# Moving the mixing of a channel group from the values' tile into the first tile of the next head pair's period

## The chip, the cores and the metric

One core of a Trainium2 chip runs the kernel. The metric is device time in microseconds. TensorE (PE) multiplies matrices, VectorE (DVE) and ScalarE (ACT) do elementwise work, GpSimd (POOL) a little of it, SyncE (SP) issues all the DMAs of this kernel.

## What is computed

One layer of a hybrid decoder works on 1024 prompt positions and 8 x 4 sample positions, 1056 token columns in all (T). One input projection gives the rows of two branches: 16 heads of attention and 8 channel groups of a gated position mixing. The output projection follows, then the residual and a norm. Cut to what matters here:

```python
z = rms_norm(x, norm_g) @ w_in
q, k, v, ga, u, vc, gb = split(z)
vc = layer_norm(gelu(vc), ln_g, ln_b);  u = gelu(u)
o_attn = dilated_attention(rope(q), rope(k), v)
# mixing of group g: positions s of a chunk of 128 to positions t, lower triangle only
mixed = einsum('gts,bcsgk->bctgk', w_s * tril, vc_chunks) + b_s
y = x + concat([o_attn * silu(ga), u * mixed * silu(gb)]) @ w_out
```

The sample positions open a chunk of their own, so they are mixed with the first 4 x 4 corner of `w_s`.

## The kernel before

**Tiles of the projections.** `w_in` is cut into 56 tiles of 128 output columns and `w_out` into 16. A tile is computed in three chunks of 352 token columns (`proj_chunk`, L190). Operands are split into a high and a low f16 half, and a chunk is 16 x 3 = 48 matmuls of 128x128 by 352 into one of three PSUM banks called `proj`. The weights of the next tile are split in four parts by ACT and DVE (`w_split`, L145 and L146: `wh`, `wl`) from `wraw`, which SP loads in two halves (L127). One tile of PE's work takes some 21 us.

**Side work.** Every 6 matmuls `proj_chunk` calls `fill` (24 calls a tile). It runs what is due in `timeline`, a list of (position, function), where the position counts tiles from the period's start. This side work is the prompt's attention (scores L634 and L635, mask and maximum L643, transposes of the probabilities by DMA L671, products L682 and L689, `onat` L694, transpose of the result L700), the sample's attention on the cached keys and values (`kvr` loaded at L735, split into `kvh` and `kvl` on ACT L743, DVE L746 or POOL L745, scores L774, `stsb` L763 and L782, mask L797), and the mixing. A scheduler of the framework then places instructions by priority and by which buffers are free, so that what is emitted later can stand earlier; the order on each engine is fixed when the program is built. The rotation (`rope`) is emitted at a higher priority.

**Periods.** `period(p)` handles head pair p-1 (g = p-1) beside the tiles that pair p and group g need. Its tiles are G (the gate `ga` of the pair), U (`u` of the group, into the tile `gb`), B (silu of `gb`, multiplied into the same tile `gb`), V (the values of pair p), and then X and Y, the two rotated halves of the queries and keys, by `run_ab`. Period 1 has U, B, V, X, Y; periods 2 to 5 have G, U, B, V, X, Y; period 6 has G, U, V, X, Y; period 7 has G, B, V, X, Y; period 8 has G, U, B, U, B. After Y, `rope` (L484) multiplies each chunk with cosines and sines (L490 to L497, reading two `proj` banks), splits it (`qkhl`, L153 and L154), and stores it (L498, L506, L507); L512 and L516 copy the sample's columns; `stack_load` (L518) reads queries and keys back (`qst`, `khd`, `klo`).

**The mixing.** For group g, `mix_load` issues 11 DMAs: eight of the normalised rows (`vr`, L886, two buffers of four DMAs each), `vrs` (L895), the triangle's weights `wr` (L896) and the bias `bb` (L897). `mix_prep` masks and splits the weights (`wm`). `mix(g, 0)` and `mix(g, 1)` each take a `proj` bank, do 12 matmuls (L913 to L915), add the bias (L927) and multiply by `gb` (L928) on DVE, split the result into `chl` (ACT L153, DVE L154) and store it to `act_d` (L935). `mix(g, 2)` does the same for the 32 sample columns (3 matmuls, L920 to L922). It needs the tile `gb` whole, so it comes after B of its group and before U of the next one writes that tile.

**Where the mixing stands before the change.** In periods 1 to 5 `period` calls `mix_load(g)` at once and puts the four steps at the start, 0.12, 0.45 and 0.79 of the values' tile. Period 6 has none. Period 7 does so for group 5, the period before's. Period 8 mixes group 6 in its last but one and last tiles, and group 7 is mixed after the periods.

Of the kernel before, what the change touches and what calls it, by code (L numbers as in the profile page):

```python
# [23 lines left out]
NP = H // 2  # L24
# [30 lines left out]
def hybrid_step_kernel(  # L55
# [50 lines left out]
    def bank(p, tag):  # L106
        return p.tile([128, 512], F32, tag=tag, name=tag)
# [220 lines left out]
    for qd in range(4):  # L328
        p = bank(ps_p, "proj") if qd < 3 else bank(ps_o, "o")
# [10 lines left out]
    for i in range(NQ + 1):  # L340
        if i + 3 <= NQ:
            x_load(i + 3)
        t0, n = TILES[i]
# [539 lines left out]
    def vr_load(g, half):  # L883
        vr = ap_.tile([128, 4, 2, 128], F16, tag="vr", name="vr", bufs=2)
        for i in range(4):
            SP.dma_start(out=vr[:, i], in_=vr_d[half * 4 + i, :, :, g * 128:(g + 1) * 128])  # L886
        return vr

    def mix_load(g):
        vr = [vr_load(g, 0), vr_load(g, 1)]  # L890
        vrs = ap_.tile([NS, 2, 128], F16, tag="vrs", name="vrs", bufs=1)
        wr = ap_.tile([128, 160], F32, tag="wr", name="wr", bufs=1)
        bb = ap_.tile([128, 160], F32, tag="bb", name="bb", bufs=1)
        gs = slice(g * 128, (g + 1) * 128)
        SP.dma_start(out=vrs, in_=vr_d[NQ, 0:NS, :, gs])  # L895
        SP.dma_start(out=wr, in_=wst[g])  # L896
        SP.dma_start(out=bb, in_=bst[g].partition_broadcast(128))  # L897
        mixs[g] = (vr, vrs, wr, bb)

    def mix_prep(g):  # L900
        vr, vrs, wr, bb = mixs[g]
        wm = ap_.tile([128, 2, 160], F16, tag="wm", name="wm", bufs=1)
        DVE.tensor_tensor(out=wr, in0=wr, in1=trl, op=ALU.mult)
        hilo(wr, wm[:, 0], wm[:, 1], SWS)
        mixs[g] = (vr, vrs, wm, bb)
# [31 lines left out]
    def mix_steps(g, direct=False):  # L937
        return [
            (0.1, lambda: mix_prep(g)),
            (0.7, lambda: mix(g, 0, direct)),  # L940
            (0.7, lambda: mix(g, 1, direct)),
            (0.1, lambda: mix(g, 2, direct)),
        ]
# [24 lines left out]
    def period(p):  # L968
        g = p - 1
        pr, ahl = prompt_steps(g)  # L970
        tiles = []
        if g > 0:
            tiles.append((MG[g], ga_evac))
        if p < NP - 1:
            tiles.append((MU[g], u_evac))
        if p < NP - 2:
            tiles.append((MGB[g], gb_evac))
        if p == NP - 1:
            tiles.append((MGB[g - 1], gb_evac))
        if p == NP:  # L980
            tiles += [(MU[g - 1], u_evac), (MGB[g - 1], gb_evac), (MU[g], u_evac), (MGB[g], gb_evac)]
        n = len(tiles)
        if p < NP:
            tiles.append((MV[p], v_evac(p)))
            n = len(tiles) + 2
        end = n - 0.85 if p < NP else n - 0.5
        ev = at(pr, 0.65, end)
        s0 = 0.4 if g == 0 else 0.0
        ev += [(s0 + t * (n - s0), f) for t, f in sample_steps(g, ahl)]
        mg = None  # L990
        if p < NP - 2:
            mg = g
        elif p > NP - 2:
            mg = g - 1
        if mg is not None:
            mix_load(mg)
            if p < NP:
                ready = len(tiles) - 1
                pos = (ready - 0.02, ready + 0.12, ready + 0.45, ready + 0.79)
            else:  # L1000
                pos = (2.95, 3.06, 3.4, 3.72)
            ev += [(t, f) for t, (_, f) in zip(pos, mix_steps(mg))]
        if p < NP:
            ev += at(v_trs(p), end + 0.25, end + 0.5)
        ev.sort(key=lambda e: e[0])
        timeline.extend(ev)
        now[0] = 0.0
        for i, (m, evac) in enumerate(tiles):
            w_load(m + 2)
            last = p == NP and i == n - 1  # L1010
            if last:
                mix_load(g)
            sp = [(i + 0.15 + 0.2 * q, lambda q=q: w_split(m + 1, q)) for q in range(4)]
            if p == NP or i < len(tiles) - 1:
                timeline.extend(sp)
            else:
                timeline.extend([(i + 0.15 + 0.2 * q, lambda q=q: w_split(MA[p], q)) for q in range(4)])
            timeline.sort(key=lambda e: e[0])
            for ci, (c0, w) in enumerate(CHUNKS):
                evac(proj_chunk(m, c0, w), c0, w)  # L1020
                if last:
                    if ci == 2:
                        while timeline:
                            timeline.pop(0)[1]()
                    act_load(slice(0, 7), c0, w)
                    act_load(slice(8, 15), c0, w)
        if p < NP:
            w_load(MB[p] + 1)
            for q in range(4):
                w_split(MB[p], q)  # L1030
            run_ab(p, None)
        assert not timeline
        now[0] = None
        if p == NP:
            for c0, w in CHUNKS:
                act_load(slice(7, 8), c0, w)

    for p in range(1, NP + 1):
        period(p)
# [294 lines left out]
```

## Time and profile before

| | |
|---|---|
| median of three runs | 1815.75 us (1815.25 to 1816.78) |
| the profiled execution | 1814.15 us |
| its span | 1812.2 us |
| its mean granted TensorE clock | 0.997 |
| busy in it: PE, DVE, ACT, POOL | 1778.8, 1069.9, 719.1, 118.1 us |

The span reaches from the first instruction of the profiled execution to the last; its time has some 2 us around that. Matmuls are pipelined: a row's duration is longer than the distance to the next one, so PE's pace is read from the starts. A row of a timeline has the start, the duration, the engine, the line of the kernel, the operation, its output and inputs, and in brackets how long the engine had been idle and what released it. Waits are listed as engine and instruction, then what ended the wait: total us, times, longest.

The periods begin, by the trace, at about 292 (period 1), 446, 600, 754, 907, 1060 (period 6), 1190 (period 7) and 1325 us (period 8); the first of the tiles' matmuls run some microseconds ahead of that, beside the rotation's end.

### The profile page before, as it was taken

How to read it: one execution, taken by the hardware profiler on the slowest of the kernel's cores; microseconds unless marked ns; L12 is line 12 of the kernel's file. 1: busy time of each engine (PE TensorE's matmuls, PEld its weight loads, DVE VectorE, ACT ScalarE, POOL GpSimd, SP SyncE). 2: the span in 40 equal slices, each digit the busy share in tenths (PEclk: the TensorE clock that was granted, in tenths of full speed). 3: DMA queues.
4: the chain of work that ended last, by engine and by line, in shares of the span. 5: the costliest groups of instructions: out<-in, count | busy, mean ns of one | idle time of the engine just before them, and what ended most of it. 6: DMA issues, size and time to landing. Idle time of an engine off the chain costs nothing. (4 is left out here: it accounts for less than half of the span.)

```text
span 1812.2 us, 37265 instructions
## 1 busy us (share of the span) xinstructions
PE 1778.8 (98%) x15040; PEld 1223.4 (68%) x15040; DVE 1069.9 (59%) x2383; ACT 719.1 (40%) x1605; POOL 118.1 (7%) x139
## 2 busy tenths in 40 slices
PE   8999999999999999999999999999999999999997
PEld 7866666666666666666666666666666666666677
DVE  7733595775766576477557657657657533434343
ACT  7522322642543444254344345445345311312133
POOL 0000020110010010001001000001001000000001
PEclk9999999999999999999999999999999999999999
DMA  7443337786667658567767866767765992333314
GB/s 269 104 102 70 78 116 213 160 183 179 160 141 171 166 123 197 157 158 149 174 157 143 176 182 150 177 189 160 185 177 124 241 340 79 71 79 80 81 42 192
DMA packets 340415, 276.13 MB, mean 152 GB/s; under 512 B 255890, under 2 KB 291730, under 8 KB 338130
## 3 DMA queue, kind: packets, MB, share of 16 engines
q1 hardware_dynamic: 340242, 273.76, 59.7%
q8 instruction: 117, 1.92, 0.4%
q14 instruction: 56, 0.45, 0.1%
HBM read 179.85 MB, written 38.26 MB: 120 GB/s over the span
## 5 line engine op out<-in xcount | busy, mean ns | idle before, releaser
L196 PE MATMUL proj<-xh,wh 128*128 128x352 f16 (+3 forms) x3712 | 1106.5, 302 | 4.2 <-ACT wh L145 1.2
L196 PE MATMUL proj<-xl,wh 128*128 128x352 f16 (+3 forms) x3712 | 1106.1, 302 | 1.4 <-DVE xl L154 1.4
L196 PE MATMUL proj<-xh,wl 128*128 128x352 f16 (+3 forms) x3712 | 1105.9, 302 | 0.3 <-DVE wl L146 0.3
L196 PEld LDWEIGHTS <-wh 128*128 128x128 f16 x7424 | 696.4, 98 | 324.1 <-issue 4.4
L196 PEld LDWEIGHTS <-wl 128*128 128x128 f16 x3712 | 362.3, 98 | 172.2 <-issue 1.7
L146 DVE SCALAR_TENSOR_TENSOR wl<-wraw,wh 128x512 f16<-128x512 f32 x288 | 191.7, 693 | 136.0 <-ACT wh L145 135.9
L145 ACT ACTIVATE wh<-wraw 128x512 f16<-128x512 f32 x288 | 167.3, 620 | 184.3 <-PE proj L196 178.8
L746 DVE SCALAR_TENSOR_TENSOR kvl<-kvr,kvh 128x896 f16<-128x896 f32 x128 | 142.2, 1111 | 69.7 <-ACT kvh L743 53.5
L655 ACT ACTIVATE sp<-sp,mn 128x256 f32<-128x256 f32 (+7 forms) x128 | 99.0, 774 | 169.7 <-DVE mn L643 169.7
L154 DVE SCALAR_TENSOR_TENSOR pn<-sp,pn 128x512 f16<-128x512 f32 (+2 forms) x192 | 111.9, 593 | 66.4 <-ACT pn L153 65.4
L745 POOL TENSOR_SCALAR kvh<-kvr 128x896 f16<-128x896 f32 x64 | 63.5, 993 | 781.0 <-DVE r L662 338.7
L153 ACT ACTIVATE pn<-sp 128x512 f16<-128x512 f32 (+2 forms) x192 | 96.7, 518 | 42.3 <-DMA pt<-pn 36.2
L743 ACT ACTIVATE kvh<-kvr 128x896 f16<-128x896 f32 x64 | 60.4, 944 | 85.2 <-issue 37.2
L643 DVE CUSTOM_DVE_ANT_0 sp<-s,mp 128x512 f32<-128x512 f32 (+3 forms) x128 | 74.7, 584 | 24.0 <-PE s L635 24.0
L154 DVE SCALAR_TENSOR_TENSOR yhl<-proj,yhl 128x352 f16<-128x352 f32 (+1 forms) x42 | 21.4, 510 | 84.0 <-ACT yhl L153 84.0
L153 ACT ACTIVATE yhl<-proj 128x352 f16<-128x352 f32 (+1 forms) x42 | 18.7, 446 | 125.6 <-PE proj L196 96.5
L682 PE MATMUL o<-vst,pt 128*128 128x128 f16 x576 | 66.1, 220 | 1.4 <-DVE onat L694 1.3
L634 PE MATMUL s<-khd,qst 128*128 128x512 f16 (+2 forms) x192 | 62.6, 326 | 3.0 <-DVE mn L643 2.9
L689 PE MATMUL o<-vst,pt 128*128 128x64 f16 x576 | 62.7, 193 | 0.0
L635 PE MATMUL s<-klo,qst 128*128 128x512 f16 (+2 forms) x192 | 60.2, 326 | 0.6 <-DMA klo<-k_d 0.6
L693 ACT ACTIVATE ot<-o,r 128x64 f32<-128x64 f32 x128 | 38.7, 302 | 42.4 <-PE o L689 42.3
L682 PEld LDWEIGHTS <-pt 128*128 128x128 f16 x576 | 52.5, 99 | 4.0
(191 smaller groups left out, 1505.2 us busy)
## 6 DMA issues: line engine op xcount, KB each, us to landing
wraw<-in_w_in SPq DMA_DIRECT2D x110, 512.0 KB, 4.8
kvr<-in_kc SPq DMA_DIRECT2D x64, 448.0 KB, 3.8
kvr<-in_vc SPq DMA_DIRECT2D x64, 448.0 KB, 3.8
wraw<-in_w_out SPq DMA_DIRECT2D x32, 512.0 KB, 4.9
yn<-in_x SPq DMA_DIRECT2D x8, 1024.0 KB, 12.9
out_y_p<-yn SPq DMA_DIRECT2D x16, 512.0 KB, 3.5
xn<-in_x SPq DMA_DIRECT2D x7, 1024.0 KB, 6.2
out_v_o<-tb SPq DMA_DIRECT2D x24, 176.0 KB, 3.7
```

The costliest lines, as they stand in the source:

```text
L145: ACT.activation(out=hi[:, sl, :], in_=r[:, rs, :], func=AF.Copy, scale=WS)
L146: DVE.scalar_tensor_tensor(out=lo[:, sl, :], in0=r[:, rs, :], scalar=WS, in1=hi[:, sl, :], op0=ALU.mult, op1=ALU.subtract)
L153: ACT.activation(out=hi, in_=src, func=AF.Copy, scale=scale)
L154: DVE.scalar_tensor_tensor(out=lo, in0=src, scalar=scale, in1=hi, op0=ALU.mult, op1=ALU.subtract)
L196: PE.matmul(out=ps[:, 0:n], lhsT=a[:, k, :], rhs=b[:, k, c0:c0 + n], start=(i == 0), stop=(i == 3 * KT - 1))
L634: PE.matmul(out=ps[:, 0:n], lhsT=qst[h][:, tq], rhs=khd[h][:, j0:j0 + n], start=True, stop=False)
L643: DVE.tensor_tensor_reduce(sp[:, j0:j0 + n], ps[:, 0:n], mp[:, S - nk + j0:S - nk + j0 + n], 1.0 / (QS * KS), prev, ALU.add, ALU.min, mn,)
L655: ACT.activation(out=sp[:, 0:nk], in_=sp[:, 0:nk], func=AF.Exp, scale=-1.0, bias=prev, accum_out=den)
L682: PE.matmul(out=o[:, 0:128].rearrange("p (l c) -> p l c", l=2), lhsT=pt[:, j], rhs=vst[:, :, kb, h * HD:(h + 1) * HD], start=(kb == 0), st ...
L689: PE.matmul(out=o[:, 0:64], lhsT=pt[:, w + j], rhs=vst[:, 0, kb, h * HD:(h + 1) * HD], start=False, stop=(kb == nb - 1))
L745: POOL.tensor_scalar(hi, r, VS, 1.0, ALU.mult, ALU.mult)
L746: DVE.scalar_tensor_tensor(out=lo, in0=r, scalar=KS if j < DB else VS, in1=hi, op0=ALU.mult, op1=ALU.subtract)
```

## The change

```diff
-        mg = None
-        if p < NP - 2:
-            mg = g
-        elif p > NP - 2:
-            mg = g - 1
-        if mg is not None:
-            mix_load(mg)
-            if p < NP:
-                ready = len(tiles) - 1
-                pos = (ready - 0.02, ready + 0.12, ready + 0.45, ready + 0.79)
-            else:
-                pos = (2.95, 3.06, 3.4, 3.72)
-            ev += [(t, f) for t, (_, f) in zip(pos, mix_steps(mg))]
+        if 1 <= g <= NP - 3 or p == NP:
+            m0 = g - 1 if g <= NP - 3 else NP - 3
+            ev += [(t, f) for t, (_, f) in zip((0.02, 0.07, 0.4, 0.73), mix_steps(m0))]
+        if g <= NP - 4 or p == NP - 1:
+            ev.append((n - 2.3, lambda: mix_load(g if g <= NP - 4 else NP - 3)))
+        if p == NP:
+            ev.append((1.2, lambda: mix_load(NP - 2)))
+            ev += [(t, f) for t, (_, f) in zip((2.95, 3.06, 3.4, 3.72), mix_steps(NP - 2))]
```

Groups 0 to 4 are now mixed in the G tile of periods 2 to 6, and group 5 in that of period 8, each with its steps at 0.02, 0.07, 0.4 and 0.73 of the tile. Their loads are called 0.7 into the values' tile of the period before (n counts the tiles with X and Y). In period 8 the loads of group 6 are called at 1.2 and its mixing stays. Nothing else is edited; lines behind 987 stand 5 lower. What is computed is the same.

The order of the built program shows what the scheduler made of it. The first place is DVE in the values' tile of period 1, behind the split of a weight part (`wl`, L146). Before, with the first part of the mixing of group 0 (L927, L928 and `chl`) among scores, probabilities (`pn`) and weights:

```order
L927 SCALAR_TENSOR_TENSOR proj<-proj,bb 128x512
L782 TENSOR_TENSOR stsb<-v,sa 128x4x7x8
L928 TENSOR_TENSOR proj<-proj,gb 128x512
L662 RECIPROCAL r<-den 128x1
L154 SCALAR_TENSOR_TENSOR pn<-sp,pn 128x512
L154 SCALAR_TENSOR_TENSOR pn<-sp,pn 128x128
L154 SCALAR_TENSOR_TENSOR chl<-proj,chl 128x512
L146 SCALAR_TENSOR_TENSOR wl<-wraw,wh 128x512
```

And now:

```order
L782 TENSOR_TENSOR stsb<-v,sa 128x4x7x8
L146 SCALAR_TENSOR_TENSOR wl<-wraw,wh 128x512
L662 RECIPROCAL r<-den 128x1
L146 SCALAR_TENSOR_TENSOR wl<-wraw,wh 128x512
L154 SCALAR_TENSOR_TENSOR pn<-sp,pn 128x512
L154 SCALAR_TENSOR_TENSOR pn<-sp,pn 128x128
L746 SCALAR_TENSOR_TENSOR kvl<-kvr,kvh 128x896
```

Three operations of the mixing are gone from there, and the same work as before follows in nearly the same order, up to L797.

The second place is DVE at the end of the rotation's third chunk, at the start of period 2 (the same at the other five boundaries). Before, the rotation's L497 was followed by a weight part, the split `qkhl`, and the copies L512 and L516:

```order
L495 TENSOR_TENSOR ta<-proj,cos_t 128x352
L496 TENSOR_TENSOR tb<-proj,sin_t 128x352
L146 SCALAR_TENSOR_TENSOR wl<-wraw,wh 128x512
L497 TENSOR_TENSOR o_5583<-ta,tb 128x352
L146 SCALAR_TENSOR_TENSOR wl<-wraw,wh 128x512
L154 SCALAR_TENSOR_TENSOR qkhl<-o_5583,qkhl 128x704
L512 COPY qbd<-qkhl 32x16x4
L516 COPY knw<-qkhl 32x64
```

And now:

```order
L495 TENSOR_TENSOR ta<-proj,cos_t 128x352
L496 TENSOR_TENSOR tb<-proj,sin_t 128x352
L146 SCALAR_TENSOR_TENSOR wl<-wraw,wh 128x512
L497 TENSOR_TENSOR o_5531<-ta,tb 128x352
L927 SCALAR_TENSOR_TENSOR proj<-proj,bb 128x512
L146 SCALAR_TENSOR_TENSOR wl<-wraw,wh 128x512
L154 SCALAR_TENSOR_TENSOR qkhl<-o_5531,qkhl 128x704
L928 TENSOR_TENSOR proj<-proj,gb 128x512
L512 COPY qbd<-qkhl 32x16x4
L516 COPY knw<-qkhl 32x64
```

The mixing's first two operations stand on both sides of `qkhl`; its `chl` follows the eight copies, ahead of L218, the first chunk of G. On PE the 12 matmuls of part 0 now follow 18 matmuls of that tile, those of part 1 come 42 matmuls of the tile later, and those of part 2 another 48 later. By the program's semaphores the first matmul of part 0 waits for L495 of the rotation's third chunk, part 1 for `chl` of part 0, and part 2 for L218 of the tile's second chunk.

The third place is SP behind the loads of `stack_load` at the same boundary. Before:

```order
L524 DMA klo_2716<-k_d_62 64x1024
L127 DMA wraw<-in_w_in 128x1024
L671 DMA_TRANSPOSE pt<-pn 128x2x128
L735 DMA kvr<-in_kc 128x896
L671 DMA_TRANSPOSE pt<-pn 128x2x128
L735 DMA kvr<-in_kc 128x896
```

And now:

```order
L524 DMA klo_2716<-k_d_62 64x1024
L935 DMA act_d<-chl 256x1x512
L127 DMA wraw<-in_w_in 128x1024
L886 DMA vr<-vr_d 128x2x128
L671 DMA_TRANSPOSE pt<-pn 128x2x128
L886 DMA vr<-vr_d 128x2x128 x2
L935 DMA act_d<-chl 256x1x512
L886 DMA vr<-vr_d 128x2x128 x4
L735 DMA kvr<-in_kc 128x896
L935 DMA act_d<-chl 256x1x32
L671 DMA_TRANSPOSE pt<-pn 128x2x128
L895 DMA vrs<-vr_d 32x2x128
```

The loads that the code calls in the values' tile stand here, as soon as the buffers of the group before come free; the first of the eight stands ahead of L498 of the rotation's third chunk. At the start of period 1, where the buffers are free, the eight `vr` loads and their three companions stood ahead of `wraw` and of all `kvr`; now one `wraw` and two `kvr` stand ahead of them, and the others lie among further `wraw` and `kvr`.

## The prediction

> **What bounds the kernel now.** The profiled execution took 1814.15 us, its span is 1812.2; the median of the three runs is 1815.75, 1.60 above the profiled one. The sum below is made against 1814.15, and the forecast is that sum plus 1.60. On this kernel a difference of 0.2% (3.6 us) is about what a measurement can tell from none.
>
> I read the page first. It names the engine.
>
> ```profile
> span 1812.2 us, 37265 instructions
> ...
> PE 1778.8 (98%) x15040; PEld 1223.4 (68%) x15040; DVE 1069.9 (59%) x2383; ACT 719.1 (40%) x1605; POOL 118.1 (7%) x139
> ```
>
> PE works 98% of the span. The change removes no matmul, so all that it can win is PE's idle time (and time at a lower clock), and all that it can lose is new idle time. So the second view is the list of PE's waits; its columns are total, times, longest.
>
> ```profile
> PE t L700 <- DVE mn L797: 3.8, 2, 3.5
> PE s L634 <- DVE mn L643: 2.9, 5, 0.9
> ...
> PE t L700 <- DVE onat L694: 2.1, 3, 1.0
> ...
> PE o L682 <- DVE onat L694: 1.3, 3, 0.8
> PE v L774 <- DVE stsb L763: 1.2, 1, 1.2
> ```
>
> The third view cuts the span by period (1, 3 and 7; columns: stretch and length, then PE, PEld, DVE, ACT, POOL busy, granted clock, DMA share, GB/s).
>
> ```profile
> 292.00:446.30 154.30, 147.47 (x1277) 99.71 (x1276) 99.99 (x235) 67.12 (x148) 12.40 (x13) 0.99 0.74 180
> ...
> 600.30:753.60 153.30, 152.96 (x1330) 103.88 (x1329) 97.88 (x232) 65.45 (x146) 11.18 (x13) 1.00 0.65 160
> ```
> ```profile
> 1190.50:1324.60 134.10, 131.91 (x1186) 89.99 (x1185) 91.01 (x222) 61.66 (x137) 10.64 (x13) 1.00 0.71 175
> ```
>
> Period 3 leaves PE idle for 0.3 us in 153. What can be won lies in period 1 and period 7.
>
> **Removed: the mixing in the values' tile.** In period 1 the worst stall stands in that tile: PE reaches L700 at 364.4 and gets on at 367.9, when DVE has read the bank in L797. DVE works without a pause until then, and the mixing is in its queue (start, duration, what):
>
> ```profile
> 359.91 0.69 DVE L927 SCALAR_TENSOR_TENSOR proj<-proj,bb 128x512 f32<-128x512 f32 x1
> ...
> 360.92 0.69 DVE L928 TENSOR_TENSOR proj<-proj,gb 128x512 f32<-128x512 f32 x1
> ...
> 362.38 0.69 DVE L154 SCALAR_TENSOR_TENSOR chl<-proj,chl 128x512 f16<-128x512 f32 x1
> ...
> 367.22 0.64 DVE L797 CUSTOM_DVE_ANT_0 ss<-t,msk,mn 64x416 f32<-64x416 f32 x1
> ```
>
> Each of the three holds DVE some 0.63 us (start to start), 1.9 together, and the order shows none of them ahead of L797 any more. L797 then ends 1.9 sooner. PE comes sooner too, because its 12 mixing matmuls ahead of the wait are gone:
>
> ```profile
> 354.60 0.22 PE L913 MATMUL proj<-wm,vr 128*128 128x128 f16 x1
> ...
> 355.27 0.17 PE L774 MATMUL v<-qbd,kvh 128*128 128x16 f16 x1
> ...
> 592.91 0.31 PE L196 MATMUL proj<-xh,wh 128*128 128x352 f16 x1
> ...
> 595.60 0.31 PE L196 MATMUL proj<-xh,wh 128*128 128x352 f16 x1
> ```
>
> The 12 take 0.67 us. They are done elsewhere at the same price, so they change the stall and not the sum of the work. The stall becomes 3.5 - 1.9 + 0.7 = 2.3: a gain of 1.2. Bounds: nothing, if another operand holds L797; 3.5, if the queues behind it thin out as well, since the loads of vr and the stores of chl leave this tile too.
>
> The clock follows the stall:
>
> ```profile
> 364.40:367.90 3.50, 0.01 (x1) 0.00 (x0) 3.35 (x11) 2.24 (x5) 0.17 (x1) 1.00 0.66 160
> 367.90:369.10 1.20, 1.17 (x15) 0.92 (x16) 1.20 (x3) 1.20 (x4) 0.00 (x0) 1.00 0.92 191
> 369.10:372.50 3.40, 3.40 (x22) 2.40 (x20) 2.41 (x7) 1.38 (x4) 0.00 (x0) 0.50 1.56 308
> ```
> ```profile
> 321.00:324.00 3.00, 1.83 (x25) 1.22 (x23) 1.37 (x9) 1.89 (x8) 0.00 (x0) 1.00 0.44 138
> 324.00:328.00 4.00, 4.00 (x43) 2.79 (x42) 3.78 (x9) 4.00 (x10) 0.00 (x0) 1.00 0.28 50
> ```
>
> For 3.4 us the clock is 0.50, which loses 1.7 us. The drop comes 1.2 us after the gap has ended, so the stretch of the same length ahead of it (365.7 to 369.1) was idle for only 2.2 us. A gap of 1.2 (at 321.5) brought no drop. A gap of 2.3 lies between the two, so the gain is between 0 and 1.7, and I take the middle, 0.85. The Trainium skill ("TensorE: Matmul & The Clock Gate", section "What's actually happening") says that the rate halves after at least one idle window of about 3.4 us, in windows that run free of the program; by that a gap of 2.3 brings no drop, the gain is 1.7 and the sum 0.85 better. The trace agrees with the length of the slow stretch (3.4 us) but shows the drop after a window that was idle for two thirds of it, so the rule is not my value, but a rival.
>
> Two smaller waits behind the stall hang on the same backlog, as do those of L682 in the list (1.3 in all, the longest in period 5) and two in period 7, where group 5 was mixed:
>
> ```profile
> PE s L634 <- DVE mn L643: 0.6, 2, 0.4
> ```
> ```profile
> PE o L682 <- DVE onat L694: 0.8, 1, 0.8
> ```
> ```profile
> PE s L634 <- DVE mn L643: 0.9, 1, 0.9
> PE t L700 <- DVE onat L694: 0.6, 1, 0.6
> ```
>
> The first fence is 355 to 380 us, the second 907 to 1061, the third 1240 to 1324.6. I take two thirds of each, since what comes next on DVE is close behind: 0.4, 0.9 and 1.0. Bounds: nothing, and all of it (0.6, 1.3, 1.5).
>
> **Moved: the loads of group 0.** In the order, period 1 now issues weights and two key tiles ahead of them. Before, these waited 7.0 us on SP:
>
> ```profile
> 296.54 5.18 SPq L886 DMA_DIRECT2D vr<-vr_d  x8
> 301.77 0.62 SPq L895 DMA_DIRECT2D vrs<-vr_d  x1
> ...
> 303.06 0.43 SPq L897 DMA_DIRECT2D bb<-in_bst  x1
> 303.54 1.72 SPq L127 DMA_DIRECT2D wraw<-in_w_in  x1
> ```
>
> That helps a wait of 0.8 us for L643 at 318.5, whose DVE queue stands behind a late key tile:
>
> ```profile
> 316.99 0.95 ACT L743 ACTIVATE kvh<-kvr 128x896 f16<-128x896 f32 x1 [3.23 <-DMA kvr<-in_kc]
> ```
> ```profile
> 317.97 1.09 DVE L746 SCALAR_TENSOR_TENSOR kvl<-kvr,kvh 128x896 f16<-128x896 f32 x1 [2.65 <-ACT kvh L743]
> 318.98 0.28 DVE L643 CUSTOM_DVE_ANT_0 sp<-s,mp 128x128 f32<-128x128 f32 x1
> ```
>
> But the first key tile's split (0.95 on ACT, then 1.09 on DVE) now stands ahead of a quarter of the next weights (L145, L146) in both queues, so that a late key tile holds up weights.
>
> ```profile
> kvr<-in_kc SPq DMA_DIRECT2D x64, 448.0 KB, 3.8
> ```
>
> Issued near 298, it lands near 302 (3.8 us in the page's list of DMAs); its split costs PE between nothing and its own 2.0. I take the gain of 0.8 less 0.4, so 0.4 (bounds 2.0, with L774's wait of 1.2 gone too, and -1.2).
>
> **Added: mixing in the first tile of the next period, at six places** (starts of periods 2 to 6 and 8). Its first matmul now follows 18 matmuls of that tile, so at 595.60 in period 3 (0.149 us each from 592.91). The bank that it is given is the one that the rotation's third chunk reads in L495:
>
> ```profile
> 593.11 0.53 DVE L491 TENSOR_TENSOR tb<-proj,sin_t 128x352 f32<-128x352 f32 x1 [4.15 <-PE proj L196]
> ...
> 595.27 0.52 DVE L495 TENSOR_TENSOR ta<-proj,cos_t 128x352 f32<-128x352 f32 x1
> ...
> 598.16 0.89 DVE L154 SCALAR_TENSOR_TENSOR qkhl<-o,qkhl 128x704 f16<-128x704 f32 x1 [0.30 <-ACT qkhl L153]
> ...
> 600.77 0.52 DVE L218 SCALAR_TENSOR_TENSOR sg<-ta,proj 128x352 f32<-128x352 f32 x1 [0.21 <-ACT ta L217]
> ```
>
> L495 ends at 595.79: PE waits 0.19, and some 0.05 to be told (L797 ended at 367.86, PE went on at 367.9): 0.24. Queued behind it on PE are all the matmuls of the tile, so this is on the path: 6 x 0.24 = 1.4 (bounds 0 and 0.5 each, 3.0). DVE's own part of the mixing is hidden: L927 and the others fill pauses, and push qkhl to 598.6 at most. The second part waits until chl of the first has been split, which I reckon for 602.2 (598.6 + 0.9 for qkhl, 1.5 for the copies between it and L218, 0.6 for L928, 0.6 for chl), against PE's arrival at 595.60 + 0.24 + 0.67 + 42 x 0.149 = 602.8: 0.6 to spare. The third has about the same. If that cover is gone, each microsecond past it is paid six times.
>
> On SP, 11 loads and 3 stores move to the tile in which the rotated keys are stored and read back:
>
> ```profile
> L886 SPq DMA_DIRECT2D vr<-vr_d x64: 524/602/1985, 296.5 to 1416.4; - x64
> ```
>
> At 0.6 us each, the stores counted like the loads, that is 8.4 us of SP's time per boundary. By the order one load stands ahead of the stores of queries and keys; it waits for the first part's matmuls (596.5), and those stores have nothing to store before qkhl is split. Seven loads and two stores stand ahead of the first cached key tile, some 5.4 us. The stores of chl are read in the last projections only. PE has spare time there: its first use of the stored keys is pushed by the mixing itself (0.9 at each part). I cost this at nothing, bounds 0 and 1 us a boundary (6).
>
> **The sum:** gains 1.2 + 0.85 + 0.4 + 0.9 + 1.0 + 0.4 = 4.75; cost 1.4. Net -3.35: profiled 1810.8, median 1812.4.
>
> **Rivals.** (a) *The stall moves and little is won.* DVE's work in that tile is the same but for 1.9 us, and L797 waits for the scores as well; then the 3.5 and the clock's drop stay (2.05 of the gain), and the net is -1.3: 1814.4. For it: DVE is busy for 3.35 of the 3.5 us. Against it: the order puts nothing else ahead of L797. (b) *Slower: the chain of the mixing misses the bank at the boundaries.* Place: the second and third part in the first tile of six periods. L927 waits for PE, stands ahead of qkhl on DVE, and ACT must split too; from 0.6 us beyond my reckoning on, PE stands. At 0.7 us on either part, 6 x 1.4 = 8.4, net +5.05: 1820.8. For it: the margins are only reckoned, and SP's and ACT's queues are new there. Against it: DVE is idle for 4.15 us ahead of L491, so it has no backlog there. (c) *The whole stall goes* with the lighter queues: 2.3 more of stall and 0.85 of clock, net -6.5: 1809.2. (d) *No drop at a gap of 2.3*: the clock slows only after a gap longer than 2.3 us, which the rows (a drop at 3.5, none at 1.2) allow; 0.85 better, 1811.6. That is the Trainium skill's rule above. (e) *The change doesn't do what it says:* the loads are put into the values' tile in the code, but the order has them in the next period's first tile. Had they stood where the code says, SP would have 11 x 0.6 = 6.6 us less there; since that is costed at nothing, the time is that of the forecast, and its chance is within it.
>
> **How the numbers follow.** Forecast 0.30, (d) 0.20, (a) 0.23, (b) 0.13, (c) 0.14. The bound of faster is 1812.1: (c), (d) for the most part (0.17) and less than half of the forecast (0.13) give 0.44. (a) and the rest of the forecast and of (d), 0.43, lie within 0.2%. (b), 0.13, is slower. The range goes from (c), rounded down to 1809.0, to (a) with its boundary waits at their bound (3.0 in place of 1.4, so 1816.0) and half a microsecond for SP's queue: 1816.5. (b) is left out, and of (c) what lies beyond its own sum.
>
> **What would show it.** In the changed profile: PE's wait at L700 in period 1's values' tile near 2.3 us, and the granted clock behind it; a wait of 0.2 at L913 with releaser L495 near 595 and its five fellows; no wait at the second and third part; L682 and L700 gone from periods 5 and 7. It is wrong if the list of waits has L913 or L634 above 0.5 us each at the boundaries, or if the stall of period 1 is as long as it was.

## The result and the profile after

The changed kernel took 1824.85 us (median of six runs, 1822.17 to 1827.81), the kernel before 1815.5 in the same comparison (1814.24 to 1816.98). The ratio is 1.0051 [1.0040, 1.0061]: slower by 0.5%, 9 us, where 1812.4 had been forecast, and above the whole range of the forecast. Each ratio here and below is against runs of the kernel before in the same session; it is not the quotient of the two medians, from which it differs by up to 0.07%. Of the runs of the experiments below, one of e4 (3126.87 us, mean granted clock 0.60) and one of e13 (2296.14 us, 0.75) are left out of medians and ratios. The profiled execution took 1823.0 us, its span is 1821.2; the table and rows below are from it, against the 1812.2 of before.

The first lines of the page say where not to look: PE does the same 15040 matmuls, in 1780.3 us against 1778.8, so most of the 9 us is time in which it is idle.

```profile
span 1821.2 us, 37243 instructions
...
PE 1780.3 (98%) x15040; PEld 1223.1 (67%) x15040; DVE 1071.6 (59%) x2383; ACT 719.5 (40%) x1605; POOL 119.8 (7%) x139
```

The list of PE's waits (total, times, longest) says at which instructions.

```profile
PE t L700 <- DVE onat L694: 8.6, 7, 2.5
PE t L700 <- DVE mn L797: 3.3, 2, 1.8
PE o L682 <- DVE onat L694: 2.7, 3, 1.6
...
PE s L634 <- DVE mn L643: 2.3, 4, 1.5
PE v L774 <- DVE stsb L763: 2.1, 1, 2.1
```

The longest wait for L797 fell from 3.5 to 1.8 (2.3 had been forecast), but waits of L700 for `onat`, 2.1 us in all before, are 8.6 now, and L682's grew from 1.3 to 2.7 instead of going. A list of waits does not say in which period they lie, so the span is cut where each period's first projection matmul starts (us; the last column takes out the mixing's own PE time, which left the V tiles and came to the first tiles: 1.61 = 0.67 + 0.67 + 0.27 a group, and the wait of 0.24 that the six boundaries gained). The row of period 8 reaches to the end of the first tile of the output projection.

| stretch | before | after | difference | without the moved mixing |
|---|---|---|---|---|
| up to period 1 | 298.17 | 299.23 | +1.06 | +1.06 |
| period 1 | 140.80 | 138.82 | -1.98 | -0.37 |
| periods 2 to 5 | 614.64 | 616.55 | +1.91 | +0.95 |
| period 6 | 129.55 | 134.63 | +5.08 | +3.23 |
| period 7 | 134.06 | 134.32 | +0.26 | +1.87 |
| period 8 | 158.40 | 161.11 | +2.71 | +0.86 |

The six boundaries' waits, 1.46, make the sum 9.1, against 9.0 between the spans. The stretch up to period 1 scattered between 297.8 and 299.25 over all kernels of this study, though none changed it. A row of the table is one profile against one, and rows scatter: with its work unchanged, period 1 took 140.8 to 143.9 us in the seven profiles in which group 0 was not moved. So the question is what happened in periods 6 and 7, and why period 1 gave so little.

**Period 6.** The DVE timeline of its second tile has an instruction of the mixing that forecast and sum had not looked at.

```profile
1084.71 0.41 DVE L154 SCALAR_TENSOR_TENSOR pn<-sp,pn 128x256 f16<-128x256 f32 x1
...
1088.22 0.33 DVE L903 TENSOR_TENSOR wr<-wr,trl 128x160 f32<-128x160 f32 x1 [3.10 <-DMA wr<-in_wst]
1088.47 0.55 DVE L643 CUSTOM_DVE_ANT_0 sp<-s,mp 128x384 f32<-128x384 f32 x1
...
1090.25 0.28 DVE L694 SCALAR_TENSOR_TENSOR onat<-o,r,ot 128x64 f32<-128x64 f32 x1
```
```profile
1085.10 0.33 PE L635 MATMUL s<-klo,qst 128*128 128x384 f16 x1
...
1090.58 0.33 PE L700 MATMUL t<-eye_t,onat 128*128 128x128 f32 x1 [1.57 <-DVE onat L694]
```
```profile
1081.75 0.61 SPq L886 DMA_DIRECT2D vr<-vr_d  x1
1083.79 0.60 SPq L895 DMA_DIRECT2D vrs<-vr_d  x1
1084.44 0.57 SPq L897 DMA_DIRECT2D bb<-in_bst  x1
1085.07 0.42 SPq L896 DMA_DIRECT2D wr<-in_wst  x1
```

L903, the mask of the next group's triangle, stands in DVE's queue long ahead of its use, and its load is the last of the eleven on SP, issued at 1085.07 and landed at 1088.2. DVE stands for 3.10 us; the scores of L635 were done by 1085.4, but L643, which reads them, is behind L903. `onat` is 1.57 us late for PE. A second wait of L700, 1.27 us at 1157.80 and also for `onat`, makes most of the rest of the period's loss. Over the kernel:

```profile
DVE wr L903 <- DMA wr<-in_wst: 6.0, 3, 4.5
```
```profile
DVE wr L903 <- DMA wr<-in_wst: 16.6, 8, 3.6
```

The first line is of before (three waits), the second of after: all eight masks wait now.

**Period 7**, X tile: PE stands 2.50 us at L700 (1292.12), where before had no wait. ACT, DVE and SP of after around it:

```profile
1286.77 0.63 ACT L153 ACTIVATE pn<-sp 128x512 f16<-128x512 f32 x1
...
1288.78 0.63 ACT L153 ACTIVATE pn<-sp 128x512 f16<-128x512 f32 x1 [1.38 <-DMA pt<-pn]
```
```profile
1281.06 1.09 DVE L746 SCALAR_TENSOR_TENSOR kvl<-kvr,kvh 128x896 f16<-128x896 f32 x1
...
1289.44 0.69 DVE L154 SCALAR_TENSOR_TENSOR pn<-sp,pn 128x512 f16<-128x512 f32 x1 [1.31 <-ACT pn L153]
1290.05 1.82 DVE L746 SCALAR_TENSOR_TENSOR kvl<-kvr,kvh 128x896 f16<-128x896 f32 x1
1291.79 0.27 DVE L694 SCALAR_TENSOR_TENSOR onat<-o,r,ot 128x64 f32<-128x64 f32 x1
```
```profile
1282.18 0.33 SPq L735 DMA_DIRECT2D kvr<-in_vc  x1
1282.82 8.61 SPq L671 DMA_TRANSPOSE pt<-pn  x4
```

And the same place before, some 4.2 us earlier in the span, ACT, DVE and SP:

```profile
1282.58 1.15 ACT L153 ACTIVATE pn<-sp 128x512 f16<-128x512 f32 x2
```
```profile
1275.83 1.08 DVE L746 SCALAR_TENSOR_TENSOR kvl<-kvr,kvh 128x896 f16<-128x896 f32 x1
```
```profile
1275.26 2.00 SPq L735 DMA_DIRECT2D kvr<-in_vc  x2
1278.65 8.01 SPq L671 DMA_TRANSPOSE pt<-pn  x4
```

Read from the end: `onat` is late because DVE did `pn` at 1289.44 and then 1.82 us of `kvl` (1.09 at 1281.06; GpSimd's split L745 ran beside it from 1289.68 to 1290.92, and whether that made it longer was not tried). `pn` was late because ACT's half of it waited 1.38 us for a buffer that a transposing DMA still read. Before, both halves ran in one piece. The transposes differ in what runs beside them: SP's row of the last 448 KB load of `kvr` ends 0.31 us ahead of theirs now (1282.51 to 1282.82), and ended 1.39 us ahead before (1277.26 to 1278.65). That load waits for `kvl` L746 to free a buffer, and `kvl` (1281.06; before 1275.83, which is 1280.0 when shifted by 4.2) is 1.1 us later against the transposes. No mixing stands on DVE there any more: with its work gone from the V tile, the scheduler placed this `kvl` behind L662 instead of ahead of it.

**Boundaries and period 1.** A boundary is as forecast (start of period 3, PE): the spacing from the last projection matmul to L913 is 0.39, 0.24 more than the usual 0.149.

```profile
594.90 0.31 PE L196 MATMUL proj<-xh,wl 128*128 128x352 f16 x1
595.29 0.22 PE L913 MATMUL proj<-wm,vr 128*128 128x128 f16 x1
```

Period 1's waits are these, of after; the 3.5 of before at L797 is 1.8, and L774's wait of 1.2 is 2.1:

```profile
PE v L774 <- DVE stsb L763: 2.1, 1, 2.1
PE t L700 <- DVE mn L797: 1.8, 1, 1.8
PE s L634 <- DVE mn L643: 1.7, 2, 1.5
PE t L700 <- DVE onat L694: 0.6, 1, 0.6
```

The drop of the clock left 369 and came at 325, behind the wait of L774 (stretch and length, PE, PEld, DVE, ACT, POOL busy, granted clock):

```profile
321.60:325.00 3.40, 1.31 (x22) 0.87 (x20) 1.74 (x10) 1.69 (x7) 0.00 (x0) 1.00 0.12 24
325.00:328.40 3.40, 3.40 (x15) 1.83 (x14) 2.97 (x5) 3.40 (x8) 0.00 (x0) 0.50 0.31 60
...
366.00:369.40 3.40, 1.71 (x19) 1.29 (x20) 1.49 (x6) 1.38 (x3) 0.17 (x1) 1.00 1.23 218
```

### The profile page after: what moved, and what is told of

It is laid out like the page before. It is cut to its first block, busy times and chain, and to the rows that moved or that the text cites. A ratio compares the mean times of both kernels' runs of the same rounds, so it can differ in the third digit from the quotient of the medians.

```text
span 1821.2 us, 37243 instructions
## 1 busy us (share of the span) xinstructions
PE 1780.3 (98%) x15040; PEld 1223.1 (67%) x15040; DVE 1071.6 (59%) x2383; ACT 719.5 (40%) x1605; POOL 119.8 (7%) x139
## 5 line engine op out<-in xcount | busy, mean ns | idle before, releaser
L146 DVE SCALAR_TENSOR_TENSOR wl<-wraw,wh 128x512 f16<-128x512 f32 x288 | 192.0, 696 | 136.1 <-ACT wh L145 135.9
L746 DVE SCALAR_TENSOR_TENSOR kvl<-kvr,kvh 128x896 f16<-128x896 f32 x128 | 142.5, 1113 | 63.0 <-ACT kvh L743 53.4
L745 POOL TENSOR_SCALAR kvh<-kvr 128x896 f16<-128x896 f32 x64 | 65.2, 1019 | 786.0 <-PE v L775 438.0
L643 DVE CUSTOM_DVE_ANT_0 sp<-s,mp 128x512 f32<-128x512 f32 (+3 forms) x128 | 74.6, 583 | 14.8 <-PE s L635 14.2
L682 PE MATMUL o<-vst,pt 128*128 128x128 f16 x576 | 66.2, 220 | 2.7 <-DVE onat L694 2.7
L634 PE MATMUL s<-khd,qst 128*128 128x512 f16 (+2 forms) x192 | 62.8, 327 | 2.5 <-DVE mn L643 2.3
L635 PE MATMUL s<-klo,qst 128*128 128x512 f16 (+2 forms) x192 | 60.1, 327 | 0.0
L662 DVE RECIPROCAL r<-den 128x1 f32<-128x1 f32 x128 | 20.5, 160 | 67.1 <-ACT sp L655 66.7
```

What stands on the lines that cost most here:

```text
L146: DVE.scalar_tensor_tensor(out=lo[:, sl, :], in0=r[:, rs, :], scalar=WS, in1=hi[:, sl, :], op0=ALU.mult, op1=ALU.subtract)
L634: PE.matmul(out=ps[:, 0:n], lhsT=qst[h][:, tq], rhs=khd[h][:, j0:j0 + n], start=True, stop=False)
L643: DVE.tensor_tensor_reduce(sp[:, j0:j0 + n], ps[:, 0:n], mp[:, S - nk + j0:S - nk + j0 + n], 1.0 / (QS * KS), prev, ALU.add, ALU.min, mn,)
L682: PE.matmul(out=o[:, 0:128].rearrange("p (l c) -> p l c", l=2), lhsT=pt[:, j], rhs=vst[:, :, kb, h * HD:(h + 1) * HD], start=(kb == 0), st ...
L745: POOL.tensor_scalar(hi, r, VS, 1.0, ALU.mult, ALU.mult)
L746: DVE.scalar_tensor_tensor(out=lo, in0=r, scalar=KS if j < DB else VS, in1=hi, op0=ALU.mult, op1=ALU.subtract)
```

## The experiments

**Which group costs.** For seven kernels (e2, e3, e5, e6, e8 and, with further edits, e12 and e15) `period` was rewritten so that a tuple names the groups that are moved; the others stay as before (the load of a group that stays behind a moved one is called at 0.75 of the period's first tile). `pm` says that the period before's group is moved, `mg` is the period's own:

```diff
+        MOVED = (0, 1, 2, 3)
+        if pm:
+            ev += [(t, f) for t, (_, f) in zip((0.02, 0.07, 0.4, 0.73), mix_steps(pg))]
...
+            elif mg in MOVED:
+                ev.append((n - 2.3, lambda: mix_load(mg)))
+            else:
+                if pm:
+                    ev.append((0.75, lambda: mix_load(mg)))
...
+                pos = (ready - 0.02, ready + 0.12, ready + 0.45, ready + 0.79)
```

Groups 0 to 3, groups 4 and 5, the change once more, then groups 5, 4 and 0 alone were expected to do this:

> Only groups 0 to 3 are moved (periods 1 to 5); groups 4 and 5 are loaded and mixed where they were. By the traces' difference, tile by tile, periods 1 to 5 ahead of group 4 gain 0 to 1 us (2.0 less in period 1, then 0.4, 0.7, -0.1). Theories D and H: about the time of the kernel before, 1814.5 to 1816.5. If the loss were spread evenly over the boundaries (0.24 us of waiting at each and some more), it would be 1818 to 1820.

> Only groups 4 and 5 are moved (to the first tiles of periods 6 and 8); groups 0 to 3 stay where they were. Theory D: the whole loss is here, 1823 to 1825. Theory H: L903 of the next group still stands in period 6 behind 10 loads, so 1.6 of it are that; also 1822 to 1825. If the loss came from period 1 or from all boundaries alike: 1816 to 1818.

> The changed kernel as it is, with a second profile. Its time should repeat, 1822 to 1828. What is looked for is which of TensorE's gaps repeat: theories H and D expect those near 322 (L774), 1089, 1276 and 1381 (L700) again at the same places and sizes; theory J expects those behind a late transposing DMA (1157 with 1.3 us and 1290 with 2.5 us) at other sizes or gone.

> Only group 5 is moved, from period 7's values' tile to period 8's first tile. Theory K (collision): with the mixing gone from there, one split of a cached tile (kvl, L746) is placed some 5 us later on VectorE; it frees the buffer of the next load (448 KB), which now starts 0.6 us ahead of the transposing DMAs, and TensorE waits 2.5 to 2.8 us at L700 near 1290 us (0 in the kernel before), with 1.7 us of slow clock where that falls so. K expects half of the loss here: 1819 to 1821, and that gap in the profile. If period 6 alone makes the loss (theory H or D for group 4): 1816 to 1817.

> Only group 4 is moved, from period 5's values' tile to period 6's first tile. Theory H: L903 of the next group is placed on VectorE in period 6 behind late loads, 1.6 us at L700 near 1089, and the boundary's 0.24: 1817.5 to 1819. Theory D (density) expects more than these two, with waits at other places of period 6: 1819 to 1822.

> Only group 0 is moved, from period 1 to period 2's first tile. The prediction's terms for that (1.2 of stall, 0.4 to 1.7 of clock, 0.4 behind it, 0.4 at the start, less 0.24 at one boundary) give 2 to 3 us less than before: 1813 to 1814. Theory M (the stall moves): period 1's idle time was 6.8 us before and is 6.4 to 7.0 in the changed kernel's profiles, in other places; M expects the clock's part alone, 1815 to 1816.5.

| moved | median us | ratio to before | period 6 | period 7 |
|---|---|---|---|---|
| 0 to 3 | 1817.9 | 1.0009 [1.0000, 1.0017] | 130.79 | 135.36 |
| 4 and 5 | 1823.98 | 1.0037 [1.0024, 1.0051] | 136.46 | 135.93 |
| 0 to 5 (the change again) | 1823.15 | 1.0037 [1.0024, 1.0050] | 133.38 | 136.33 |
| 5 | 1822.03 | 1.0027 [1.0018, 1.0036] | 129.55 | 134.08 |
| 4 | 1818.83 | 1.0016 [1.0003, 1.0028] | 133.92 | 132.72 |
| 0 | 1815.8 | 0.9995 [0.9984, 1.0005] | 129.55 | 134.04 |

Groups 0 to 3, 4 and 5 cost 0.09, 0.16 and 0.27%, together 0.52%; the change itself was measured at 0.51 and 0.37%, and groups 4 and 5 together at 0.37. So the parts add up to the whole within their intervals, and group 5, one of six, makes half of it or more, above what was expected of it. For groups 0 to 3 alone the time was expected to stay (1814.5 to 1816.5); 1817.9 is above that. Group 4 alone lengthens period 6 by 4.4 us, of which 1.85 are the mixing and its wait. Group 0 alone, where the largest gain had been forecast, brings nothing that can be measured; its interval reaches from a gain of 2.9 us to a loss of 0.9. The wait at L700 in period 7's X tile is there whenever group 5 is moved and the sample's steps stay, here with group 5 alone (with the V tile's wait, two in all; the `kvl` ahead of that load is 1.1 us later, as shown above for the change, and not the 5 that were expected):

```profile
PE t L700 <- DVE onat L694: 3.5, 2, 2.4
```

**The mask on GpSimd** (e1). With L903 on an engine that has little queued, DVE cannot stand behind the late load.

```diff
-        DVE.tensor_tensor(out=wr, in0=wr, in1=trl, op=ALU.mult)
+        POOL.tensor_tensor(out=wr, in0=wr, in1=trl, op=ALU.mult)
```

> The changed kernel with one operation on another engine: the triangle's mask of the mixing weights (L903) is done by GpSimd instead of VectorE. TensorE's and SyncE's orders stay as they are. Theory H (head of the line): L903 is placed on VectorE well ahead of its use, waits there for the load of wr (16.6 us in all in the changed kernel, 6.0 before), and the scores' maximum L643 stands behind it. H expects TensorE's 1.6 us at L700 near 1089 us and most of the 2.1 us at L774 near 322 us to go, the slow clock after the latter too: 3 to 5 us faster than the changed kernel, so 1820 to 1822. Theory D (dense periods: the loss comes from mixing in periods 6 and 8, whose side work is already dense, whatever stands in front of it) and theory J (scatter of the transposing DMAs) expect less than 1 us.

1821.26 us, ratio 1.0035 [1.0022, 1.0048]. DVE waits nowhere at L903. In period 6 the 1.57 at L700 are gone; of that stretch remains

```profile
PE o L682 <- DMA pt<-pn: 0.6, 1, 0.6
```

Period 6 took 132.29 (with e9 and e10 below, which have the mask there too: 133.01, 131.86), against 133.38 to 136.46 in the six profiles of this study with group 4 moved and the mask on DVE (the change, e3, e4, e6, and e7 and e13 below; mean 134.5): about 2 us of its loss. In the whole time, which lies where it was expected, that is not told apart from the change's two measurements, 1.0051 and 1.0037.

**The sample's value steps earlier in period 7** (e7). The sample's second half is called 0.12 of a tile sooner, so that `kvl` and the loads that it releases come ahead of the transposes again.

```diff
-        ev += [(s0 + t * (n - s0), f) for t, f in sample_steps(g, ahl)]
+        ev += [(s0 + t * (n - s0) + (-0.12 if p == NP - 1 and t > 0.5 else 0.0), f) for t, f in sample_steps(g, ahl)]
```

> The changed kernel with the sample's value steps of period 7 set 0.12 of a tile earlier, so that kvl stands between the two maxima L643 on VectorE, as it did before the change, and the 448 KB load starts some 5 us ahead of the transposing DMAs. Theory K expects the wait of 2.5 to 2.8 us near 1290 to be under 1 us and the time 2 to 4 us below the changed kernel, 1820 to 1822. If the transposing DMAs are late by themselves: no gain.

1817.54 us, 1.0008 [0.9998, 1.0018]: most of the loss is gone by one number in one period, more than was expected. Period 7 takes 130.75 instead of 134.32 and 136.33, and the X tile's wait of 2.5 us is 0.4:

```profile
PE t L700 <- DVE onat L694: 0.4, 1, 0.4
```

**Both** (e9), and **both with the mixing later in the first tile** (e10), behind 24 matmuls instead of 18, so that L495 has read the bank by then:

```diff
-            ev += [(t, f) for t, (_, f) in zip((0.02, 0.07, 0.4, 0.73), mix_steps(m0))]
+            ev += [(t, f) for t, (_, f) in zip((0.1, 0.13, 0.45, 0.75), mix_steps(m0))]
```

> The changed kernel with two edits: the mask L903 on GpSimd, and the sample's value steps of period 7 set 0.12 of a tile earlier. Theories H and K together: what each gave alone is added up, so period 6 takes some 132.3 us instead of 133 to 136 and period 7 131 instead of 134 to 136, and the time is within 1.5 us of the kernel before: 1814.5 to 1817. If one cause stood behind both (theory D, density), the second edit would give nothing beyond the first: 1817.5.

> As e9, and the mixing's steps in the first tile at 0.1, 0.13, 0.45 and 0.75 instead of 0.02, 0.07, 0.4 and 0.73, so that its first matmul follows 24 matmuls instead of 18. The boundary's wait of 0.24 for L495, six times, was a term of the prediction: it should go, 1.4 us less than e9. If part 1 or 2 then misses its bank, the gain is less, with waits at L913 or L920 in the list.

e9: 1818.67 us, 1.0008 [1.0000, 1.0017], above what was expected and no better than e7 alone; in its period 6 L700 waits 1.4 us though DVE never stood at L903, so the mask is not the only thing that makes `onat` late there. e10: 1816.44 us, 0.9997 [0.9988, 1.0005], 2.2 less than e9, against the 1.46 of the six boundary waits, which are gone. With all three mends the change is even with before, not ahead of it.

**Is it the order on DVE, or the load beside the transposes?** e11 gives the kernel before the new order of `kvl` and L662 in period 7, by value steps 0.02 earlier:

```diff
-        ev += [(s0 + t * (n - s0), f) for t, f in sample_steps(g, ahl)]
+        ev += [(s0 + t * (n - s0) + (-0.02 if p == NP - 1 and t > 0.5 else 0.0), f) for t, f in sample_steps(g, ahl)]
```

> The kernel before, its mixing untouched, with the sample's value steps of period 7 set 0.02 of a tile earlier. That alone turns VectorE's order there into that of the changed kernel: kvl (L746) behind L662. Theory K expects TensorE's wait of 2.4 to 2.8 us at L700 near 1286 and 2 to 4.5 us more than before: 1818 to 1820.5. If the moved mixing is what makes the wait, nothing changes: 1815 to 1816.5.

1815.97 us, 0.9992 [0.9983, 1.0000]; period 7 132.05, no wait at that L700. Against what was expected, the new order and the close load together are not enough for the wait: the load stands as close ahead of the transposes here as in the changed kernel (0.65 us from start to start, 0.64 there), and ACT waits only 0.33:

```profile
1279.07 0.33 SPq L735 DMA_DIRECT2D kvr<-in_vc  x1
1279.72 8.00 SPq L671 DMA_TRANSPOSE pt<-pn  x4
```
```profile
1284.62 0.63 ACT L153 ACTIVATE pn<-sp 128x512 f16<-128x512 f32 x1 [0.33 <-DMA pt<-pn]
```

The next two leave PE's, DVE's and ACT's orders up to L700 as they are and move traffic only. e13 is the changed kernel with the one load of `kvr` held until the transposes are issued (a copy of one column that needs the `onat` before it, and a later call). e14 is the kernel before with a store of 448 KB that nobody needs, issued ahead of the same transposes; with it the last load of `kvr` too stands closer to them, 0.99 us ahead instead of 1.72:

```diff
+            if (p, j) == (6, 15):
+                DVE.tensor_copy(t[:, 0:1], last_on[0][:, 0:1])
             SP.dma_start(out=t, in_=src[p, :, j % DB])
...
+        if p == NP - 1:
+            ev.append((3.75, lambda: late.pop(0)()))
```
```diff
+    scr = dram.tile([128, 896], F32, name="scr")
...
             stt[i][2] = r
+            if (p, i) == (6, 14):
+                SP.dma_start(out=scr, in_=sp[:, 0:896])
```

> The changed kernel with one load moved: in period 7 the last tile of cached values (448 KB), which starts 0.6 us ahead of the transposing DMAs, is made to wait for the attention's result (one copy of a column on VectorE ahead of it) and so follows them. The orders of the four compute engines up to L700 stay as in the changed kernel, the mixing too. Theory K (the load slows the transposing DMAs, the next probabilities wait for their buffer, and onat stands behind these on VectorE) expects the wait of 2.4 to 2.8 us near 1290 to be under 1 us, period 7 at 131.5 to 133 us and 2 to 5 us less than the changed kernel: 1819 to 1822. If VectorE's changed order is the cause by itself: no gain.

> The kernel before with one DMA more: in period 7 a store of 448 KB of probabilities to a scratch array, issued by SyncE just ahead of the transposing DMAs; the orders of the compute engines are unchanged. Theory K expects the wait at L700 near 1286 to appear, 1 to 2.5 us, and 1 to 4 us more than before: 1817 to 1820. If traffic doesn't matter there: no wait, 1815 to 1817.

e13: 1820.98 us, 1.0021 [1.0011, 1.0032]; period 7 132.60. e14: 1818.58 us, 1.0012 [1.0002, 1.0022]; period 7 136.79 instead of 134.06, with a stretch of 3.4 us at half the clock behind the wait. ACT's second half of `pn` and PE's wait, first of e13, then of e14 (their lines have moved by one to three):

```profile
1285.56 0.63 ACT L153 ACTIVATE pn<-sp 128x512 f16<-128x512 f32 x1 [0.38 <-DMA pt<-pn]
```
```profile
PE t L703 <- DVE onat L696: 0.8, 1, 0.8
```
```profile
1288.30 0.63 ACT L154 ACTIVATE pn<-sp 128x512 f16<-128x512 f32 x1 [2.46 <-DMA pt<-pn]
```
```profile
PE t L703 <- DVE onat L697: 2.8, 1, 2.8
```

Taking the transfer away takes ACT's wait from 1.38 to 0.38 and PE's from 2.50 to 0.8; adding one to the kernel before takes them from nothing to 2.46 and 2.8. That traffic close ahead of the transposes makes a part of the wait is so shown from both sides. That it is not the whole is shown by e11, where the load stood as close, and by what e13 has left.

The traces show what else differs. ACT's second half waits for the landing of the first of the four transposes, and among their packets in the changed kernel runs a packet of 16 KB that belongs to a queue of instructions and not to SP's DMAs (the list of DMA queues from 1284.76, the transposes' first packet, to that landing at 1288.76):

```profile
q8 instruction: 1, 0.02, 1.8%
```

In e11 and in before it had come ahead of the transposes' first packet. All times in the table but the last two columns count from the issue of the transposes (us):

| | last load issued | first packet | instruction packet behind it | first one landed | ACT waits | PE waits |
|---|---|---|---|---|---|---|
| before | -1.72 | 1.27 | no | 4.34 | 0 | 0 |
| e11 | -0.65 | 2.01 | no | 4.87 | 0.33 | 0 |
| e13 | none | 1.17 | yes | 4.94 | 0.38 | 0.8 |
| e6 | -1.70 | 1.32 | yes | 5.45 | 0.89 | 0.8 |
| the change | -0.64 | 1.94 | yes | 5.94 | 1.38 | 2.5 |

So the close load goes with a start some 0.7 us later, and the packet with some 1 us more from the first packet to the landing: 3.1 and 2.9 without it, 3.8, 4.1 and 4.0 with it. Each alone leaves PE a wait of at most 0.8 in these profiles, both together 2.5 (2.4 to 2.8 in the four other profiles that move group 5 and leave the steps). In e14 that packet came ahead of them too; the store and the load beside them make it 2.73 to the first packet and 7.00 to the landing. No run moved the instruction packet alone, so its part is read from the traces and not shown by an experiment.

**What is left of the idea.** e12 moves only the two groups for which a stall had been seen, 0 and 5, with the mask on GpSimd and the value steps of periods 6 and 7 earlier by 0.12; e15 adds e10's positions; e16 has those two mends and moves nothing.

> Only groups 0 and 5 are moved (those of periods 1 and 7, where TensorE idled), the mask L903 is on GpSimd, and the value steps of periods 6 and 7 are set 0.12 of a tile earlier. Theories K and H expect the gain that was forecast for period 7 (1.4 us less in e7) without the collision in period 7 and the smaller one in period 6: 1812.5 to 1815, faster than both kernels.

> Groups 0 and 5 moved, mask on GpSimd, value steps of periods 6 and 7 set 0.12 of a tile earlier (as e12), and the mixing's steps in the first tile at 0.1, 0.13, 0.45 and 0.75 (as e10). The two boundaries' 0.24 should go: 0.5 us less than e12, 1813.5 to 1815, faster than both kernels.

> The kernel before, with nothing moved: only the mask of L903 on GpSimd, and the value steps of periods 6 and 7 called 0.12 of a tile earlier. The best version so far (groups 0 and 5 moved, with these two edits and the mixing later in the first tile) took 1811.69 us against 1816.13 before. If its gain of 4.4 us comes from moving groups 0 and 5 (V-tile stalls taken out of periods 1 and 7), this kernel stays at 1814.5 to 1816.5. If the two edits alone make it, 1811 to 1813. Period 7 tells most: 134 before, 129.6 in the best version; at 132 or more here the moved group makes that gain, at 130 the earlier value steps do.

| | median us | ratio to before | period 1 | period 7 | period 8 |
|---|---|---|---|---|---|
| e12 | 1814.36 | 0.9984 [0.9974, 0.9994] | 138.05 | 129.99 | 161.44 |
| e15 | 1811.69 | 0.9974 [0.9962, 0.9985] | 139.01 | 129.55 | 161.13 |
| e16 | 1814.04 | 0.9984 [0.9975, 0.9993] | 141.24 | 131.83 | 158.96 |

e15 beats both kernels, by more than was expected. But e16, with the mixing where it was, gains as much as e12, and its interval overlaps e15's. Its median is outside both ranges that were expected, and its period 7, 131.83, stands between them, since 1.61 of mixing in it had not been counted: 130.2 without it, against 132.45 before and 129.55 in e15, so the earlier value steps make 2.2 us of that period's gain of 2.9, and PE waits nowhere in 80 us of it (the stretch as above):

```profile
1240.00:1320.00 80.00, 79.88 (x707) 54.26 (x706) 56.45 (x128) 33.90 (x71) 6.61 (x6) 1.00 0.74 178
```

From period 1 to 8 the two profiles differ by 0.4 us (1173.5 for e15, 1173.9 for e16). Whether moving groups 0 and 5 adds anything to the mends is not settled: the ratios differ by 0.1%, 1.8 us, and their intervals overlap.

## Why the prediction was wrong

None of the prediction's own signs of being wrong came: the boundaries wait as forecast, and the stall of period 1 is shorter. But L682 and L700 did not go from periods 5 and 7, as they should have, and the loss came where it had not looked. Of the 12.4 us between the forecast of -3.35 for the profile and the +9.0 that came, by the table of periods, 3.2 lie in period 6, 2.9 in period 7, 2.5 in period 1, 1.9 in periods 2 to 5, and 1.9 in period 8 and in the stretch up to period 1, which no edit touched.

**The step that failed** is that what stays behind in an emptied tile stays as it is, and "I cost this at nothing" for SP. In period 7 the prediction took two thirds of the V tile's waits as a gain of 1.0. It named no instruction of the next tile, and none of the loads that the sample's steps release. With the mixing out of the tile the scheduler put one `kvl` behind L662, its load came 1.1 us closer to four transposes, a packet of the instruction queue fell among them, and the period lost 1.87 us (3.9 in the second measurement of the change) instead of gaining. The V tile's own waits did not go either: of the 4.3 us of waits in that stretch 2.5 are new, and 1.8 stand for the 1.5 of before.

**The mask**: the eleven loads were costed at nothing because their time on SP, 0.6 us each, seemed to have room. It has, for SP. But L903 stands in DVE's queue ahead of the scores, and the last of those loads is what it waits for: 16.6 us in all, 3.10 of it in period 6. The prediction asked who waits for SP, not who is queued behind the one that waits. The bound of 1 us a boundary (6 in all) would have held period 6's 3.23 within the sum of them; it did not hold it at one boundary.

**Period 1**: the stall at L797 was forecast at 2.3 and is 1.83, so the three DVE instructions were rightly counted. But the sum for the period, 1.2 + 0.85 + 0.4 + 0.4 = 2.85, came to 0.37 in the pair of profiles. That pair shows too little, since before has the shortest period 1 of the seven profiles in which group 0 is not moved (mean 142.0); the eleven in which it is moved take 138.0 to 140.7 (mean 138.9). Without the 1.61 of mixing the means differ by 1.4, half of the sum. PE's idle time in the period hardly fell, from a mean of 7.2 us to 7.0: some 75 us into it L634 waits 0.5 to 2.0 us in the eleven (1.46 in the changed kernel's profile) and at most 0.45 in the seven, and in that profile L774 waits 2.09 behind an L903 that stood 3.61 us. So for the stall rival (a), that it moves, is right, and the terms for waits (1.2, 0.4 and 0.4) are the ones that failed here. The clock's term did come: all seven have slow stretches in period 1, and six of the eleven have none. Group 0 alone gains 0.05%, with an interval that takes in no change and these 1.4 us as well. **L682** was to lose 0.9 of its 1.3, all in periods 3 to 5; it waits 2.7 now, in periods 2, 3 and 5. Why was not tried.

**Right**: the boundaries. The first part waits 0.244 us six times, 1.46 against 1.4, and e10, without that wait, is 2.2 faster by the medians. Parts two and three wait nowhere: `chl` of part one is split 0.8 us ahead of PE (0.6 forecast), so rival (b), the one way to slower that had been written out, did not happen. The time of 1820.8 that it named was nearer than the forecast for another reason.

**The clock**: the middle, 0.85, stood for not knowing whether a gap of 2.3 brings a drop. In this kernel the gap of 2.09 did and the one of 1.83 did not; the rows above have PE idle for 2.09 of the stretch ahead of the drop, and for 1.69 of the one that holds the second gap. Rival (d), no drop at 2.3, is not borne out.

What stays open: the second wait of L700 in period 6, which has not been followed up, 0.9 us more in period 8, and as much over periods 2 to 5; the last two are within what single profiles of these kernels scatter by.

## What to carry to other kernels

Where a scheduler places instructions, taking work out of a full queue changes the order of what remains: look in the new order at the next tile too, and at which loads the moved buffers release there. Of each moved load ask which instruction waits for it, on which engine's queue that stands, and what is behind it; an early place in an in-order queue is no gain when the data is late. And before moving work away from a stall, try moving the stalled chain by a tenth of a tile: here that and the mask on GpSimd (e16) gave as much as the same with two groups moved (e12).

## What the runs showed of the hardware

The clock's slow stretches of 3.41 us (in two places two in a row) begin on a fixed grid within a run, and each drop follows one stretch of the same length in which PE was partly idle. In the 18 profiles there are 19 drops between 300 us and the last tiles; that idle time was 1.76 to 3.28 us, and stretches with up to 1.91 brought none. The change's second measurement has such a drop behind the wait in period 7 (2.64 of 3.40 us idle), which makes 1.7 of the 2.0 us by which its period 7 is longer than the first's:

```profile
1287.20:1290.60 3.40, 0.76 (x18) 0.66 (x15) 3.31 (x6) 0.26 (x2) 1.39 (x1) 1.00 0.81 151
1290.60:1294.00 3.40, 3.40 (x21) 1.99 (x18) 3.40 (x9) 1.41 (x3) 0.00 (x0) 0.50 0.47 135
```

The Trainium skill ("TensorE: Matmul & The Clock Gate", section "What's actually happening") has the rate halved after at least one idle window of about 3.4 us, in windows that run free of the kernel. The length and the grid agree with these traces; the idle part does not, since half a window is enough here.

The transposing DMAs of period 7 were held up by what ran beside them. With a load of 448 KB issued 0.64 us ahead, the first packet of four transposes moved 1.9 to 2.1 us behind their issue (six profiles); with that load held back, or 1.7 us and more ahead, 1.2 to 1.3 (five profiles). With a 16 KB packet of an instruction queue among their packets, the first transpose took 3.8 to 4.3 us from there to its landing (eight profiles), and 2.9 to 3.2 without (three). A store of 448 KB put among the loads in the kernel before kept ACT waiting 2.46 us for the transposes' buffer, where it had not waited.
